# Attention on TensorE: the transposes of each block of probabilities are handed out one at a time between long products, from a queue, and the products with the values follow from it

## The chip, the cores and the metric

The kernel runs on one core of one Trainium2 chip. The metric is the device time of one execution in microseconds (us), lower is better. One execution was also taken with the hardware profiler; all rows below come from that one.

## The reference

Two layers of a decoder over 512 tokens of width 1024. A layer has five attention branches (each four heads of 64), a gate per branch, an output projection with a layer norm, and a mixture of 16 experts.

```
...
    h = x @ w_in
...
    o_sb = merge_heads(stick_breaking_attention(heads(q, N_SB_HEADS), heads(k, N_SB_HEADS), heads(v, N_SB_HEADS)))
...
    o_moba = merge_heads(moba_attention(heads(q, N_MOBA_HEADS), heads(k, N_MOBA_HEADS), heads(v, N_MOBA_HEADS),
                                        alibi_slopes(N_MOBA_HEADS)))
    o_mla = mla_attention(c_q, c_kv, k_rope_in, g_cq, g_ckv, w_uq, w_ukv)
    o_nsa = nsa_attention(heads(q_nsa, N_NSA_HEADS), kv_nsa, g_nsa, nsa_pe, w_phi_k1, w_phi_k2, w_phi_v1, w_phi_v2,
                          alibi_slopes(N_NSA_HEADS))
    o_mem = memory_cross_attention(q_mem, mem, w_mem_kv)
    merged = jnp.zeros_like(x)
    for i, o in enumerate((o_sb, o_moba, o_mla, o_nsa, o_mem)):
        gate = jax.nn.sigmoid(x @ w_gate[i] + b_gate[i])
        merged = merged + gate * (o @ w_br[i])
    return merged @ w_out
```

Four of the branches end in a softmax over the scores, times the values; stick-breaking attention has products of `1 - sigmoid` along the row in the softmax's place.

## The kernel before, in words

**Numbers.** Every matrix product is made of three products: each operand is split into a high part, rounded to the fast 32-bit format of TensorE, and a low part that holds the rest. ScalarE (ACT) makes the high part, `hi` (L97 is its plain copy), and VectorE (DVE) the low one, `lo` (L112). Tiles of the program are named by their tag: `xh`, `xl` are the two parts of the residual stream, `wh` those of a weight, `oh` those of a branch's output, `bh` those of its projection.

**A head.** In each branch a head has four blocks of 128 queries. `score_block` (L239) multiplies queries and keys into a PSUM bank `s` (there are two). DVE adds the distance term and takes the row's minimum into an SBUF tile `ne` (L254; there are three of them, `BUFS["ne"]`), ACT takes the exponential (L259), DVE the reciprocal of the sum (L260) and the scaling (L262, or L264 with a gate). Where there is no distance term, the minimum is read from `s` and the exponential goes from `s` to `ne`. Stick-breaking uses two `ne` tiles for each block: a mask (L425), tanh on ACT (L427), a linear step (L428), a scan along the row (L432) and a difference (L433), back in the first tile.

**Turns.** `to_pt` (L267) then turns the block over, since the product with the values needs the keys on the partitions: one transpose of 128x128 for every 128 keys (L124, `tr`), one to four a block, into a PSUM bank `pt` (two). I call such a transpose a turn. ACT's copy into `pth` (L97) and DVE's difference into `ptl` (L112) split the bank. When a head's four blocks are turned, `causal_pv` multiplies them with the values into the one PSUM bank `pv`, and `pv_out` adds its two halves (L280 on ACT, L281 on DVE).

**The order.** A head alone would leave TensorE waiting for DVE and ACT, so each of the five stages (memory, stick-breaking, MoBA, MLA, NSA) weaves three generators: `a`, the attention of this branch, a step for each query block; `g`, the gates and the projection of the branch before (L780 to L800: gate product `f<-xh,wh` from `fm_tile` L166, then `f<-oh,bh`); and `q`, the queries, keys and values of the branch behind. A string of letters for each stage (`orders`, L1642) says whose turn it is, and `weave` (L867) calls them. That is the order in which the program is written. A list scheduler then emits, for each engine, the instruction that is ready by its own estimate, with the place in the written order as its priority. So each engine's order comes out of the scheduler, and every engine executes its own in order.

There are 472 turns of `ne` blocks in the two layers.

Of the kernel before, what the change touches and what calls it, by code (L numbers as in the profile page):

```python
# [18 lines left out]
P = 128  # L19
D = 1024  # L20
S = 512
NT = 4
KT = 8
# [47 lines left out]
class Trunk:  # L71
    def __init__(self, tc, A, C, out, dbg=None, upto=None):
        self.tc, self.nc, self.A, self.C, self.out = tc, tc.nc, A, C, out
        self.dbg, self.upto = dbg or {}, upto
        self.uid = 0

    def nm(self, s):
# [36 lines left out]

    def mm(self, out, lhsT, rhs, start, stop):
        self.nc.tensor.matmul(out, lhsT, rhs, start=start, stop=stop)  # L116

# [41 lines left out]
    def fm_tile(self, wh, wl, M=P, N=S, x=None, cut=1):  # L159
        o = self.ps("f")  # L160
        xh, xl = (self.xh, self.xl) if x is None else x
        for c in range(cut):
            n = slice(c * N // cut, (c + 1) * N // cut)
            for k in range(KT):
                for m, (a, b) in enumerate(((wh, xh), (wh, xl), (wl, xh))):
                    self.nc.tensor.matmul(o[:M, n], a[:, k, :M], b[:, k, n], start=c + k + m == 0, stop=k == KT - 1 and m == 2,  # L166
                                          skip_group_check=cut > 1)
        return o
# [8 lines left out]
    def tm_chunk(self, w, c0, use, x=None, nt=NT, outer="k"):  # L177
# [5 lines left out]
        def part(g, kk, t):  # L183
            if g not in hl:
                hl[g] = self.split_w(self.load_w(w[512 * g : 512 * g + 512, c0 : c0 + 256].rearrange("(k p) c -> p k c", p=P), (4, 256)))
            h, l = hl[g]
            k = 4 * g + kk
            sl = slice(t * P, (t + 1) * P)
            d = o[t // 2][:, 256 * (t % 2) : 256 * (t % 2) + 256]
            for m, (a, b) in enumerate(((xh, h), (xh, l), (xl, h))):  # L190

                self.nc.tensor.matmul(d, a[:, k, sl], b[:, kk, :], start=k == 0 and m == 0 and t % 2 == 0,  # L192
                                      stop=k == KT - 1 and m == 2, skip_group_check=True)
        its = [(g, kk) for g in range(2) for kk in range(4)]
# [120 lines left out]
    def causal_head(self, passes, vt, strip=0, slope=1.0):  # L315
        pt = self.pt_tiles()
        for i in range(NT):
# [3 lines left out]
            yield  # L321
        pv = self.ps("pv")
        self.causal_pv(pv, pt, vt, True, True)
        return pv

# [47 lines left out]
    def mem_att(self, l, out):  # L373
        for pr in range(2):
            o32 = self.o_tile()
            out.append(o32)
            for hh in range(2):
# [7 lines left out]
                pv = self.ps("pv")  # L385
                for j in range(2):
                    for m in range(2):
                        self.mm(pv[:, :S], self.mv[j][:, h, :], pt[m][:, 512 * j : 512 * j + 512], j == 0 and m == 0, j == 1 and m == 1)
                self.pv_out(pv, o32, self.H2[hh])
                yield  # L390
# [19 lines left out]
    def sb_att(self, l, out):  # L410
        nc = self.nc
        for pr in range(2):
            o32 = self.o_tile()
            out.append(o32)
            for hh in range(2):
# [3 lines left out]
                for i in range(NT):  # L419
# [15 lines left out]
                    yield  # L435
                pv = self.ps("pv")
                self.causal_pv(pv, pt, lambda j: self.sv[j][:, h, :], True, True)
                self.pv_out(pv, o32, self.H2[hh])
                yield
# [16 lines left out]
    def moba_att(self, l, out):  # L456
        for pr in range(2):
            o32 = self.o_tile()
            out.append(o32)
            for hh in range(2):  # L460
                h = 2 * pr + hh
                q, k = self.bq[h], self.bk[h]
                pv = yield from self.causal_head(self.std_passes(q, k), lambda j: self.bv[j][:, h, :], 0, SLOPES[h])
                self.pv_out(pv, o32, self.H2[hh])
                yield
            self.dump(f"o_moba{pr}_{l}", o32)
# [132 lines left out]
    def mla_att(self, l, out):  # L599
        for pr in range(2):  # L600
            o32 = self.o_tile()
            out.append(o32)
            for hh in range(2):
# [5 lines left out]
                          (lambda sl: qb[K, sl], lambda sl: ka[K, sl])]  # L609
                pv = yield from self.causal_head(passes, lambda j: self.lv[j][:, h, :], 1)  # L610
                self.pv_out(pv, o32, self.H2[hh])
                yield
# [106 lines left out]
    def nsa_att(self, l, out):  # L719
# [32 lines left out]
        for pr in range(2):  # L752
            o32 = self.o_tile()
            out.append(o32)
            for hh in range(2):
# [3 lines left out]
                for m in range(2):  # L759
# [6 lines left out]
                    pts.append(pt)  # L766
                pv = self.ps("pv")
                self.mm(pv, self.vc[:, h, :], pc[:, 0, :], True, False)
                self.mm(pv, self.vc[:, h, :], pc[:, 1, :], False, False)
                for m in range(2):  # L770
                    self.causal_pv(pv, pts[m], lambda j, m=m: self.nv[j][:, m, :], False, m == 1)
                self.pv_out(pv, o32, self.H2[hh])
                yield
# [91 lines left out]

    @staticmethod
# [729 lines left out]
    def layer(self, l, gat, att):  # L1596
# [8 lines left out]
        with tc.tile_pool(name=f"pre{l}", bufs=1, reuse_waits="tile") as pre:  # L1605
# [6 lines left out]
            with tc.tile_pool(name=f"exp{l}", bufs=1, reuse_waits="tile") as ep:  # L1612
# [103 lines left out]
```

## Time and profile before

| | |
|---|---|
| median of 3 runs | 1697.85 us (1696.06, 1697.85, 1702.87) |
| the profiled execution | 1704.54 us, its span 1702.7 us |
| granted TensorE clock, mean | 0.972 of full speed |
| attention of layer 0, of layer 1 | about 75 to 600 us, 890 to 1440 us of the span |
| experts of layer 0, of layer 1 | the rest, from 600 and from 1440 us |

The span is the profiler's stretch from the first instruction to the last. Times within it are counted from its start. A row of the timeline is one instruction, or several of a kind in a row ("x4"), with its start, its length, and in square brackets how long its engine sat idle before it and whose work ended that. The end of a product on TensorE is modelled, and includes the time that the last columns take through the array: the next product starts before it. So what a product costs in a stream is read from start to start.

### The profile page before, as it was taken

To read this page: it belongs to the slowest core of one execution; us is meant where nothing else is said; L and a number is where in the kernel's file an instruction comes from. 1 tells how busy PE (TensorE), PEld (TensorE's weight loads), DVE (VectorE), ACT (ScalarE), POOL (GpSimd) and SP (SyncE) were. 2 spreads that over 40 slices of the span, in tenths; PEclk is the share of its full clock that TensorE was granted. 3 is DMA by queue.
4 is the path that set the end of the run, shared out by engine and by line. 5 is a ranking of instruction groups with operands and counts; after the bars stand their busy time and mean duration, and the time that the engine had idled before them with its cause. 6 is when DMAs were issued, how large, how long until landed. Compare 5 with 4: busy or idle time off the path is not lost. (4 is left out here: it accounts for less than half of the span.)

```text
span 1702.7 us, 22755 instructions
## 1 busy us (share of the span) xinstructions
PE 1603.2 (94%) x7936; PEld 1271.8 (75%) x7936; DVE 1253.3 (74%) x2551; ACT 867.3 (51%) x1655; POOL 272.7 (16%) x218
## 2 busy tenths in 40 slices
PE   8999999999999998899699999999999999989995
PEld 7877877788777786666587778777877787766673
DVE  6777658764785689988788766588557956898887
ACT  5644446343463335788346444464344624358871
POOL 0000011111112112333300000111101121223332
PEclk9999999989999998999799999999999999999997
DMA  8232222434328747997541323223332285499954
GB/s 254 64 91 77 67 71 61 119 95 124 106 79 281 255 165 282 378 379 251 195 141 52 94 73 81 66 62 98 79 88 63 58 305 183 170 326 380 381 178 156
DMA packets 254563, 273.61 MB, mean 161 GB/s; under 512 B 38666, under 2 KB 191360, under 8 KB 254432
## 3 DMA queue, kind: packets, MB, share of 16 engines
q1 hardware_dynamic: 241032, 223.98, 41.3%
q0 software_dynamic: 13312, 47.98, 8.2%
q8 instruction: 67, 1.10, 0.3%
q14 instruction: 64, 0.52, 0.1%
q10 hardware_dynamic: 88, 0.03, 0.0%
HBM read 239.18 MB, written 32.77 MB: 160 GB/s over the span
## 5 line engine op out<-in xcount | busy, mean ns | idle before, releaser
L166 PE MATMUL f<-xh,wh 128*128 128x512 f32 (+2 forms) x1920 | 631.0, 397 | 2.0 <-DVE ot L592 1.1
L166 PEld LDWEIGHTS f<-xh,wh 128*128 128x128 f32 (+1 forms) x1920 | 355.7, 189 | 77.0 <-PE f L625 1.2
L166 PE MATMUL f<-xl,wh 128*128 128x512 f32 (+2 forms) x960 | 381.1, 397 | 0.0
L112 DVE TENSOR_TENSOR wh<-rw,wh 128x1024 fp32r<-128x1024 f32 (+1 forms) x174 | 227.5, 1313 | 51.5 <-ACT wh L97 50.4
L798 POOL TENSOR_TENSOR mg<-mg,gt 128x512 f32<-128x512 f32 x64 | 96.8, 1512 | 986.1 <-DVE gt L797 986.1
L166 PEld LDWEIGHTS f<-xl,wh 128*128 128x128 f32 (+1 forms) x960 | 181.0, 188 | 36.7 <-DVE xl L112 0.2
L97 ACT CAST wh<-rw 128x1024 fp32r<-128x1024 f32 (+3 forms) x178 | 178.5, 1012 | 52.6 <-PE f L192 14.9
L788 ACT ACTIVATE gt<-f,bgh 128x512 f32<-128x512 f32 x80 | 55.0, 688 | 211.8 <-PE f L166 211.8
L116 PE MATMUL f<-wh,xh 128*112 128x512 f32 (+1 forms) x564 | 153.9, 400 | 1.9 <-DVE wh L112 1.9
L116 PE MATMUL f<-oh,bh 128*128 128x512 f32 x480 | 132.5, 403 | 0.1
L797 DVE SCALAR_TENSOR_TENSOR gt<-gt,f 128x512 f32<-128x512 f32 x64 | 43.8, 684 | 107.3 <-PE f L116 102.8
L116 PEld LDWEIGHTS f<-wh,xh 128*112 128x112 f32 (+1 forms) x564 | 98.3, 178 | 31.8 <-DVE wh L112 3.3
L97 ACT CAST pth<-pt 128x128 fp32r<-128x128 f32 (+1 forms) x192 | 77.4, 417 | 87.2 <-PE pt L124 81.5
L116 PE MATMUL f<-eh,xh 128*112 128x512 f32 (+1 forms) x396 | 110.5, 401 | 0.9 <-DVE eh L112 0.8
L112 DVE TENSOR_TENSOR ptl<-pt,pth 128x128 fp32r<-128x128 f32 (+1 forms) x192 | 88.9, 473 | 24.7 <-ACT pth L97 21.8
L116 PEld LDWEIGHTS f<-oh,bh 128*128 128x128 f32 x480 | 89.8, 191 | 20.0 <-issue 1.2
L116 PE MATMUL s<-qk,qk 128*128 128x256 f32 (+7 forms) x416 | 99.2, 336 | 5.9 <-DVE st L254 2.6
L97 ACT CAST wh<-rp 128x1024 fp32r<-128x1024 f32 x84 | 87.5, 1053 | 30.9 <-PE pt L116 16.3
L112 DVE TENSOR_TENSOR wh<-rp,wh 128x1024 fp32r<-128x1024 f32 x70 | 95.4, 1374 | 8.4 <-ACT wh L97 7.8
L124 PE MATMUL pt<-ident,ne 128*128 128x128 f32 x472 | 83.7, 279 | 8.6 <-DVE ne L433 3.8
L116 PEld LDWEIGHTS s<-qk,qk 128*128 128x128 f32 (+1 forms) x416 | 67.5, 194 | 26.9 <-DVE st L254 9.3
L124 PEld LDWEIGHTS pt<-ident,ne 128*128 128x128 f32 x472 | 54.7, 141 | 42.4 <-issue 17.1
(355 smaller groups left out, 2756.4 us busy)
## 6 DMA issues: line engine op xcount, KB each, us to landing
rp<-in_w_up_dram SPq DMA_DIRECT2D x96, 512.0 KB, 14.4
rw<-in_w_gate_dram SPq DMA_DIRECT2D x80, 512.0 KB, 3.8
rp<-in_w_down_dram SPq DMA_DIRECT2D x48, 512.0 KB, 13.6
rw<-in_w_in_dram SPq DMA_DIRECT2D x38, 512.0 KB, 3.8
rw<-in_w_out_dram SPq DMA_DIRECT2D x32, 512.0 KB, 6.5
yd<-xl POOLq DMA_DIRECT2D x28, 448.0 KB, 6.8
xl<-xd POOLq DMA_DIRECT2D x24, 448.0 KB, 7.5
rb<-in_w_br_dram SPq DMA_DIRECT2D x80, 128.0 KB, 3.3
```

What stands on the lines that cost most here:

```text
L97: return nc.scalar.copy(out, in_)
L112: return e.tensor_tensor(out, in_, hi.bitcast(F32), ALU.subtract)
L116: self.nc.tensor.matmul(out, lhsT, rhs, start=start, stop=stop)
L124: return self.nc.tensor.transpose(out, in_, self.ident[:k, :k])
L166: self.nc.tensor.matmul(o[:M, n], a[:, k, :M], b[:, k, n], start=c + k + m == 0, stop=k == KT - 1 and m == 2, skip_group_check=cut > 1)
L788: nc.scalar.activation(t, gp, AF.Tanh, bias=self.bgh[:, b * 8 + f : b * 8 + f + 1], scale=0.5)
L797: nc.vector.scalar_tensor_tensor(t, t, 1.0, bp, ALU.add, ALU.mult)
L798: i = nc.gpsimd.tensor_tensor(m, m, t, ALU.add)
```

## The change

Products now count. All that had called TensorE directly goes through `mm`, and each product of 256 columns or more (`long`) adds one to a count (`tick`). `to_pt` no longer emits a block's turns: it puts each into a queue (`later`). The first one of a block becomes due 20 long products after it was queued (`delay`), each further one 2 long products behind the one ahead of it (`space`), and after the last one of a block of nb the queue rests for max(1, 10 - 2(nb - 1)) (`gap_t`). The split into `pth` and `ptl` is issued with the last turn. The products with the values are closures (`end`, `out`) in the same queue, so they follow the turns they need. `weave` empties the queue at the end of each stage. Nothing else is computed, and the number of instructions is the same. The strings of `orders` and the scheduler stay.

```diff
-    def mm(self, out, lhsT, rhs, start, stop):
-        self.nc.tensor.matmul(out, lhsT, rhs, start=start, stop=stop)
+    def mm(self, out, lhsT, rhs, start, stop, **kw):
+        i = self.nc.tensor.matmul(out, lhsT, rhs, start=start, stop=stop, **kw)
+        if rhs.shape[-1] >= self.long:
+            self.big = i
+            self.tick()
+    def tick(self):
+        if self.busy:
+            return
+        self.now += 1
+        while self.pend and max(self.pend[0][0], self.due) <= self.now:
+            if self.do_next():
+                break
+    def do_next(self):
+        _, gap, f = self.pend.pop(0)
+        self.busy = True
+        f()
+        self.busy = False
+        self.due = self.now + gap
+        return gap
+    def flush(self):
+        while self.pend:
+            self.do_next()
+    def later(self, f, gap=0, delay=0):
+        self.pend.append((self.now + delay, gap, f))
...
     def to_pt(self, e, nb, dst):
-        t = self.ps("pt")
+        h, l = dst
+        ts = []
+        def turn(b):
+            if b == 0:
+                ts.append(self.ps("pt"))
+            t = ts[0]
+            if True:
+                self.tr(t[:, b * P : (b + 1) * P], e[:, b * P : (b + 1) * P])
+            if b == nb - 1:
+                src = t[:, : nb * P].rearrange("p (b q) -> p b q", q=P)
+                self.hi(h, src)
+                self.lo(l, src, h)
         for b in range(nb):
-            self.tr(t[:, b * P : (b + 1) * P], e[:, b * P : (b + 1) * P])
-        src = t[:, : nb * P].rearrange("p (b q) -> p b q", q=P)
-        h, l = dst
-        self.hi(h, src)
-        self.lo(l, src, h)
+            self.later(lambda b=b: turn(b), self.space if b < nb - 1 else max(1, self.gap_t - self.space * (nb - 1)), 0 if b else self.delay)
...
-                pv = self.ps("pv")
-                self.causal_pv(pv, pt, lambda j: self.sv[j][:, h, :], True, True)
-                self.pv_out(pv, o32, self.H2[hh])
+                def end(h=h, hh=hh, pt=pt, o32=o32):
+                    pv = self.ps("pv")
+                    self.causal_pv(pv, pt, lambda j: self.sv[j][:, h, :], True, True)
+                    self.pv_out(pv, o32, self.H2[hh])
+                self.later(end)
...
-    def weave(parts, order):
+    def weave(self, parts, order):
         for c in order:
             next(parts[c], None)
         for g in parts.values():
             for _ in g:
                 pass
+        self.flush()
...
+    busy = False
+    long, delay, space, gap_t = 256, 20, 2, 10
```

**What moves on TensorE.** The scheduler still reorders, so the order that comes out of it is shown at three places. Numbers behind a tag tell tiles of one tag apart.

The first place is the MoBA stage of layer 0, the third and fourth query block of a head, before the change. `s_2095` and `s_2110` are their scores, `ne_2098` and `ne_2113` their probabilities, `f_2145` a gate's product. Rows 7 and 8 below are this place in the trace.

```order
L116 MATMUL s_2095<-qk_1536,qk_1135 128x384
L116 MATMUL s_2110<-qk_1535,qk_1135 128x512
L116 MATMUL s_2110<-qk_1536,qk_1135 128x512
L116 MATMUL f_2126<-oh_2052,bh_2060 128x512 x3
L116 MATMUL f_2126<-oh_2055,bh_2060 128x512 x3
...
L166 MATMUL f_2145<-xh_102,wh_2142 128x512
L124 MATMUL pt_2104<-ident,ne_2098 128x128 x3
L166 MATMUL f_2145<-xh_102,wh_2142 128x512
L166 MATMUL f_2145<-xl_103,wh_2142 128x512
L124 MATMUL pt_2119<-ident,ne_2113 128x128 x4
L166 MATMUL f_2145<-xh_102,wh_2142 128x512 x2
```

The same two blocks with the change; their probabilities are now `ne_2093` and `ne_2104`, the gate's product is `f_2132`, and `ne_2037` is the block ahead.

```order
L117 MATMUL s_2099<-qk_1518,qk_1135 128x512
L154 MATMUL pt_2102<-ident,ne_2037 128x128
L117 MATMUL f_2110<-oh_2043,bh_2051 128x512 x2
L154 MATMUL pt_2102<-ident,ne_2037 128x128
...
L117 MATMUL f_2132<-xh_102,wh_2129 128x512
L154 MATMUL pt_2145<-ident,ne_2093 128x128
L117 MATMUL f_2132<-xh_102,wh_2129 128x512
L117 MATMUL f_2132<-xl_103,wh_2129 128x512
L154 MATMUL pt_2145<-ident,ne_2093 128x128
L117 MATMUL f_2132<-xh_102,wh_2129 128x512 x2
...
L154 MATMUL pt_2161<-ident,ne_2104 128x128
```

Where three and four turns stood in a lump, each now stands alone with one to three long products behind it. From the last score of the fourth block to that block's first turn there were 17 long products and 3 turns; now there are 28 and 5.

The second place is the stick-breaking stage of layer 0, before the change: the fourth score of a head and the turns near it.

```order
L116 MATMUL pv_1299<-ptl_1187,v_591 128x128
L124 MATMUL pt_1324<-ident,ne_1317 128x128
L116 MATMUL s_1361<-qk_960,qk_672 128x512
L116 MATMUL s_1361<-qk_961,qk_672 128x512
L166 MATMUL f_1401<-xh_102,wh_1398 128x512
L166 MATMUL f_1401<-xl_103,wh_1398 128x512
L124 MATMUL pt_1339<-ident,ne_1332 128x128 x2
```

The same score, `s_1323`, with the change. `ne_1225` is the block of 512 keys of the head ahead.

```order
L154 MATMUL pt_1357<-ident,ne_1225 128x128
L117 MATMUL f_1345<-xh_102,wh_1342 128x512 x2
L154 MATMUL pt_1357<-ident,ne_1225 128x128
...
L154 MATMUL pt_1357<-ident,ne_1225 128x128
L117 MATMUL f_1345<-xh_102,wh_1342 128x512
L117 MATMUL s_1323<-qk_917,qk_662 128x512
L117 MATMUL s_1323<-qk_918,qk_662 128x512
L117 MATMUL f_1345<-xh_102,wh_1342 128x512
```

The turns of a head's last block now run on until the scores of the next head are under way. Its `ne` tile comes free with the last of them, and one long product behind that stands a score that needs the bank which tanh empties into that tile.

The third place is the end of the NSA stage of layer 0, before the change. `pv_4943` is the stage's last product with the values; `oh_5013` and `oh_5016` are the outputs of its two pairs of heads, `oh_4015` one of the MLA stage.

```order
L116 MATMUL pv_4943<-ptl_4827,v_3813 128x128
L166 MATMUL f_4975<-xl_103,wh_4972 128x512
...
L166 MATMUL f_4975<-xh_102,wh_4972 128x512
L116 MATMUL f_5002<-oh_4015,bh_4967 128x512 x3
...
L116 MATMUL f_5056<-oh_5013,bh_5021 128x512 x3
L116 MATMUL f_5056<-oh_5016,bh_5021 128x512 x3
```

And with the change.

```order
L154 MATMUL pt_4977<-ident,ne_4717 128x128 x3
L154 MATMUL pt_4983<-ident,ne_4730 128x128 x4
L117 MATMUL f_5075<-xh_102,wh_5072 128x512 x2
...
L117 MATMUL pv_4990<-ptl_4692,v_3813 128x128
L117 MATMUL f_5075<-xh_102,wh_5072 128x512
L117 MATMUL f_5102<-oh_5013,bh_5067 128x512 x3
L117 MATMUL f_5121<-xh_102,wh_5118 128x512
...
L117 MATMUL f_5056<-oh_5016,bh_5021 128x512
L117 MATMUL f_5102<-oh_5016,bh_5067 128x512
```

The last turns come out in lumps where the queue is emptied. The last product with the values stands later among the gates' products, and 11 long products lie between it and the first that uses the second pair's output, where there were 44.

## Rows read from the trace of the kernel before

**Rows 1.** Page: busy time and share of the span, by engine.
```profile
PE 1603.2 (94%) x7936; PEld 1271.8 (75%) x7936; DVE 1253.3 (74%) x2551; ACT 867.3 (51%) x1655; POOL 272.7 (16%) x218
```

**Rows 2.** Windows, both layers' attention: length, PE, PEld, DVE, ACT, POOL busy, clock, DMA share.
```profile
75.00:600.00 525.00, 513.99 (x2487) 410.88 (x2485) 354.36 (x771) 243.77 (x525) 62.32 (x50) 0.99 0.39 116
890.00:1440.00 550.00, 540.12 (x2644) 431.69 (x2643) 375.63 (x820) 260.74 (x567) 52.24 (x33) 0.99 0.34 102
```

**Rows 3.** Tile pt, all engines: the turns, and what PE sat idle for.
```profile
L124 PE MATMUL pt<-ident,ne x472: 270/273/332, 52.1 to 1358.7; 128*128 128x128 f32 x158
...
  DVE ne L433: 3.8, 12
  DVE ne L262: 2.8, 6
```

**Rows 4.** Waits of PE, 75 to 600 us: engine, line, from whom: total us, times, longest.
```profile
PE s L116 <- ACT ne L259: 1.4, 1, 1.4
PE s L116 <- DVE st L254: 1.3, 3, 0.8
...
PE s L116 <- ACT ne L427: 0.4, 1, 0.4
```

**Rows 5.** Page, costliest groups: the score products: busy, mean | idle before.
```profile
L116 PE MATMUL s<-qk,qk 128*128 128x256 f32 (+7 forms) x416 | 99.2, 336 | 5.9 <-DVE st L254 2.6
```

**Rows 6.** Timeline of PE: one turn and four turns between long products, no wait.
```profile
84.66 0.63 PE L166 MATMUL f<-xh,wh 128*128 128x512 f32 x2
85.12 0.60 PE L124 MATMUL pt<-ident,ne 128*128 128x128 f32 x4
85.48 0.48 PE L166 MATMUL f<-xl,wh 128*128 128x512 f32 x1
85.79 0.39 PE L166 MATMUL f<-xh,wh 128*128 128x512 f32 x1
...
244.50 0.63 PE L166 MATMUL f<-xh,wh 128*128 128x512 f32 x2
244.97 0.27 PE L124 MATMUL pt<-ident,ne 128*128 128x128 f32 x1
245.00 0.48 PE L166 MATMUL f<-xl,wh 128*128 128x512 f32 x1
245.31 0.63 PE L166 MATMUL f<-xh,wh 128*128 128x512 f32 x2
```

**Rows 7.** Timeline of PE, MoBA stage of layer 0: scores to turns of two blocks.
```profile
209.80 1.55 PE L116 MATMUL f<-oh,bh 128*128 128x512 f32 x6
...
213.85 0.39 PE L166 MATMUL f<-xl,wh 128*128 128x512 f32 x1
215.03 0.63 PE L124 MATMUL pt<-ident,ne 128*128 128x128 f32 x4 [0.80 <-DVE ne L262]
```

**Rows 8.** Timeline of VectorE, the same place.
```profile
210.02 0.69 DVE L254 CUSTOM_DVE_ANT_0 ne<-s,strip 128x512 f32<-128x512 f32 x1
...
213.05 1.44 DVE L112 TENSOR_TENSOR bh<-rb,bh 128x256 fp32r<-128x256 f32 x1
214.41 0.47 DVE L262 TENSOR_SCALAR ne<-ne,st 128x512 f32<-128x512 f32 x1
```

**Rows 9.** Timeline of PE, stick-breaking stage of layer 0: a score and turns that wait.
```profile
114.13 0.62 PE L116 MATMUL s<-qk,qk 128*128 128x384 f32 x2 [0.38 <-ACT ne L427]
...
120.03 0.52 PE L124 MATMUL pt<-ident,ne 128*128 128x128 f32 x3 [0.28 <-DVE ne L433]
```

**Rows 10.** Waits of VectorE, 30 to 600 us, the one for a turned `ne` tile.
```profile
DVE ne L254 <- PE pt L124: 0.8, 1, 0.8
```

**Rows 11.** Timeline of PE, end of the MLA stage: last values product, first use of its output.
```profile
432.19 0.27 PE L116 MATMUL pv<-ptl,v 128*128 128x128 f32 x1
...
433.97 0.75 PE L116 MATMUL s<-kc,qk 128*128 128x64 f32 x6
434.78 0.50 PE L116 MATMUL f<-oh,bh 128*128 128x512 f32 x1
```

More of the change, by code (lines that the diff above doesn't have):

```diff
@@ L75, in __init__ @@
         self.uid = 0
+        self.pend, self.now, self.due, self.big = [], 0, 0, None
     def nm(self, s):
@@ L165, in fm_tile @@
                 for m, (a, b) in enumerate(((wh, xh), (wh, xl), (wl, xh))):
-                    self.nc.tensor.matmul(o[:M, n], a[:, k, :M], b[:, k, n], start=c + k + m == 0, stop=k == KT - 1 and m == 2,
-                                          skip_group_check=cut > 1)
+                    self.mm(o[:M, n], a[:, k, :M], b[:, k, n], c + k + m == 0, k == KT - 1 and m == 2, skip_group_check=cut > 1)
         return o
@@ L190, in part @@
             for m, (a, b) in enumerate(((xh, h), (xh, l), (xl, h))):
-                self.nc.tensor.matmul(d, a[:, k, sl], b[:, kk, :], start=k == 0 and m == 0 and t % 2 == 0,
-                                      stop=k == KT - 1 and m == 2, skip_group_check=True)
+                self.mm(d, a[:, k, sl], b[:, kk, :], k == 0 and m == 0 and t % 2 == 0, k == KT - 1 and m == 2, skip_group_check=True)
         its = [(g, kk) for g in range(2) for kk in range(4)]
@@ L321, in causal_head, with out @@
             yield
-        pv = self.ps("pv")
-        self.causal_pv(pv, pt, vt, True, True)
-        return pv
+        def out(use):
+            pv = self.ps("pv")
+            self.causal_pv(pv, pt, vt, True, True)
+            use(pv)
+        return lambda use: self.later(lambda: out(use))
     def std_passes(self, q, k):
@@ L384, in mem_att @@
                     yield
[L385 to L388, printed above, removed]
-                self.pv_out(pv, o32, self.H2[hh])
+                def end(h=h, hh=hh, pt=pt, o32=o32):
+                    pv = self.ps("pv")
+                    for j in range(2):
+                        for m in range(2):
+                            self.mm(pv[:, :S], self.mv[j][:, h, :], pt[m][:, 512 * j : 512 * j + 512], j == 0 and m == 0, j == 1 and m == 1)
+                    self.pv_out(pv, o32, self.H2[hh])
+                self.later(end)
                 yield
@@ L435, in sb_att, with end @@
                     yield
-                pv = self.ps("pv")
-                self.causal_pv(pv, pt, lambda j: self.sv[j][:, h, :], True, True)
-                self.pv_out(pv, o32, self.H2[hh])
+                def end(h=h, hh=hh, pt=pt, o32=o32):
+                    pv = self.ps("pv")
+                    self.causal_pv(pv, pt, lambda j: self.sv[j][:, h, :], True, True)
+                    self.pv_out(pv, o32, self.H2[hh])
+                self.later(end)
                 yield
@@ L462, in moba_att @@
                 q, k = self.bq[h], self.bk[h]
-                pv = yield from self.causal_head(self.std_passes(q, k), lambda j: self.bv[j][:, h, :], 0, SLOPES[h])
-                self.pv_out(pv, o32, self.H2[hh])
+                pv = yield from self.causal_head(self.std_passes(q, k), lambda j, h=h: self.bv[j][:, h, :], 0, SLOPES[h])
+                pv(lambda x, o32=o32, hh=hh: self.pv_out(x, o32, self.H2[hh]))
                 yield
@@ L609, in mla_att @@
                           (lambda sl: qb[K, sl], lambda sl: ka[K, sl])]
-                pv = yield from self.causal_head(passes, lambda j: self.lv[j][:, h, :], 1)
-                self.pv_out(pv, o32, self.H2[hh])
+                pv = yield from self.causal_head(passes, lambda j, h=h: self.lv[j][:, h, :], 1)
+                pv(lambda x, o32=o32, hh=hh: self.pv_out(x, o32, self.H2[hh]))
                 yield
@@ L766, in nsa_att, with end @@
                     pts.append(pt)
[L767 to L772, printed above, removed]
+                def end(h=h, hh=hh, pts=pts, o32=o32):
+                    pv = self.ps("pv")
+                    self.mm(pv, self.vc[:, h, :], pc[:, 0, :], True, False)
+                    self.mm(pv, self.vc[:, h, :], pc[:, 1, :], False, False)
+                    for m in range(2):
+                        self.causal_pv(pv, pts[m], lambda j, m=m: self.nv[j][:, m, :], False, m == 1)
+                    self.pv_out(pv, o32, self.H2[hh])
+                self.later(end)
                 yield
@@ L864, in x_tile @@
             self.lo(self.xl[:, 4 * g : 4 * g + 4, t * P : (t + 1) * P], v, h)
-    @staticmethod
-    def weave(parts, order):
+    def weave(self, parts, order):
         for c in order:
```

## The prediction, made before the changed kernel was run

> **What bounds the kernel now.** I read the page first: TensorE is busy for 94% of the span, no other engine for more than 74% [rows 1]. So only two things can shorten this kernel, fewer products, which the change doesn't bring, or less time in which TensorE stands still. Where it stands still is read next, from the windows of the two attention stretches, the only stages that the change touches: 525.0 - 514.0 = 11.0 us idle in layer 0 and 550.0 - 540.1 = 9.9 us in layer 1 [rows 2]. That is all there is to win at first sight, some 21 us of 1704.54. DVE is not full there either (354 of 525 us).
>
> Then what it stands still for. The answer on the tile pt gives the turns: 12 waits for the stick-breaking block (DVE L433), 3.8 us, and 6 for a scaled softmax block (L262), 2.8 us [rows 3]. The waits of layer 0 give the scores, which wait for a PSUM bank until the step that reads it has run: 1.4 + 1.3 + 0.4 us in 5 waits [rows 4]; in the whole run the scores stand behind 5.9 us of idle time [rows 5]. One block shows why a turn waits. Its scores are through when the next products start, at 209.80, and its probabilities are scaled at 214.41 + 0.47 = 214.88: 5.1 us, of which 1.44 is a split of a weight that DVE has in between [rows 8]. The order had put only 17 long products and 3 turns between (first place), 4.3 us at the cadence below, so TensorE idles for 0.80 us [rows 7].
>
> **The price of a turn itself.** Two long products start 0.47 us apart from the next thing, 0.235 each: 244.50 to 245.31 is 0.81 us for three of them and one turn, so the turn costs 0.11. Four turns in a lump: 84.66 to 85.79 is 1.13 us with three long products, so 0.43, again 0.11 each [rows 6]. A turn alone is no cheaper and no dearer than in a lump. So splitting the lumps as such I cost at nothing (472 turns, 0 us); what counts is where the turns stand against the work that they wait for.
>
> The Trainium skill (TensorE: Matmul & The Clock Gate, "Step-by-step" and "LDWEIGHTS") says that TensorE loads the next weights beneath the product that runs, and gives the load of 128 columns some 107 ns. By that a single turn between two long products would hide its load, and the sum would be lower, as in the last rival below. The 0.11 us of the turn at 244.97, which stood alone, speaks against it.
>
> **Part by part.**
>
> *Turns later.* What waits cost is more than their idle time, since a product's end is modelled late: the turn due at 213.85 + 0.235 = 214.08 starts at 215.03, 0.95 us late for 0.80 idle [rows 7]. With 0.15 more for each, the 18 waits are worth 6.6 + 18 x 0.15 = 9.3 us [rows 3]; that is the lower bound of what turns lose. For the upper one I went through the timeline run by run, start to start, as with the rows above: 166 runs of adjacent turns, 452 turns, the first at 52.1 and the last at 1358.7 us [rows 3], take 71.8 us beyond the products beside them, against 452 x 0.109 = 49.3: 22.5 us of delay, most of it too short to show as idle time.
>
> How much of it goes is a matter of the order. I counted, for all 196 score blocks with a turn, the products between the end of the scores and the first turn, at the cadence of the rows: the median rises from 4.7 to 7.8 us, and runs of one turn from 36 to 246. In the block shown it goes from 17 to 28 long products, 4.3 to 7.1 us, against a chain of 5.1. A quarter of the blocks does less well, since the scheduler puts a turn early where its estimate says it is ready, and lumps stay where the queue is emptied (third place). Taking for each kind of block the median chain that the timelines show (2.9 to 6.3 us), the sum of what the turns come too early falls from 43 to 16.5 us over both layers, and with chains 15% longer from 111 to 33: 62 to 70% goes. I take 60%, since a turn no longer late lets DVE and ACT meet other work, and apply it to the upper bound, because that was measured by starts and holds the lower one: **-13.5 us**; the ends are 0.62 x 9.3 = -6 and 0.70 x 22.5 = -16.
>
> *Tiles and banks held longer.* A turn that comes later holds its `ne` tile for longer, and there are three. A score block whose tile isn't free can't be read out, so its bank `s` stays full and the score after next waits. In the order 37 of 98 blocks of a layer had a tile that was freed only after their own scores; with the change 60. In the second place a score stands one long product behind the turn that frees the tile which its bank has to be emptied into; such a wait was 0.38 us before [rows 9]. Summed as above, what scores come too early grows from 16.0 to 25.6 us, by 60%. What scores lose now is 5.9 us of idle [rows 5] and, for some 10 waits, 0.15 each, so 7.4; 60% of that is **+4 us**. The ends are 0 (the tile is freed before DVE gets there) and the rival below. The bank `pt` is held for longer too, from a block's first single turn to its split; the queue rests after each block, and I cost this at nothing; without that cover it would come out as a wait of the turns, in the ends above.
>
> *Products with the values, and stage ends.* They follow the turns, so the output of a stage's last head is ready later, and the first projection that reads it stands 2.3 to 2.6 us behind the last value product in three stages instead of 2.3 to 10 (third place: 11 long products, 44 before). The trace has such a place: 432.30 to 434.78 is 2.5 us, and there the projection starts 0.15 us after its place in the stream, 433.97 and six scores of 0.11 [rows 11]. Ten stage ends in all: 0 to 1.5 us; I take **+0.5**.
>
> *What is queued behind.* ACT's copy of a turned block now stands with its last turn; behind it on ACT stand exponentials and weight splits. TensorE has work of the gates meanwhile, and I cost it at nothing. The loads on SP and POOL come out in the same number and nearly the same order, and DMA is busy for 0.39 of the time in these stretches [rows 2]: nothing.
>
> **The sum** against the profiled execution: 1704.54 - 13.5 + 4 + 0.5 = 1695.5 us. That execution is 6.7 us above the median of the runs shown, 1697.85; the difference of -9.0 carried over to the median gives **1688.9 us**. A change of 0.5%, 8.5 us, is about what a measurement of this kernel can tell from none, so the forecast is at its edge.
>
> **Rivals.** *Waits only change place.* TensorE gets the turns without a wait, but the chain of DVE and ACT is no shorter, and each score that comes after a held tile gives back what a turn gained. For it speaks the order (37 to 60 held blocks), against it that DVE has slack in attention. Gain of turns -13.5, scores as much: 1698 us.
>
> *Everything falls into place.* Turns gain their upper end, 16, and the scores, no longer delayed by a head that ran late, lose their 7.4 as well: 1697.85 - 23 = 1675. For it speaks that turns and scores wait for the same chain of DVE steps; against it the second place.
>
> *Three tiles are too few (slower).* The 46 more held blocks (23 in each layer) wait in DVE's queue for their tile, with everything behind them, and the scores at 0.62 us each, the mean of the five waits of layer 0 [rows 4]: +28.5, less 13.5, so 1713. It decides from the point where some 22 of the 46 wait at that price, 22 x 0.62 = 13.5. For it speaks the one wait of DVE for a turned tile, 0.8 us [rows 10]; against it that 37 held blocks a layer made only that one. The Trainium skill (same page, its table of the engine's figures) says that VectorE and ScalarE take their queues strictly in order, only TensorE draws loads ahead; so a wait for a tile would hold all that DVE has behind it, as this rival assumes.
>
> *The weight load hides.* A turn alone costs its own columns only, 0.235 x 128/512 = 0.06: 472 x 0.05 = 24 us more, 1665. The row of the lone turn speaks against it [rows 6].
>
> *The change doesn't do what it says*, since the scheduler moves turns back: the order excludes it, 246 single turns for 36.
>
> **How the numbers follow.** The forecast's own case 0.55, from 1682 to 1700 by its bounds; a little over half of it lies beyond 8.5 us of gain (0.30), the rest within (0.25). Waits that change place 0.20 (0.16 within, 0.04 slower). Everything falls into place 0.12. Three tiles too few 0.09 (slower). The hidden load 0.04. So faster 0.30 + 0.12 + 0.04 = 0.46, the same 0.25 + 0.16 = 0.41, slower 0.13. The range goes from 1674 to 1703: it leaves out the hidden load, most of the slower case and the tails, under 2 in 10.
>
> **What would show it.** Right: turns x1 in the timeline, the idle time before them from DVE L433 and L262 at about a third of 6.6 us, attention's PE idle time at 6 to 8 us a layer in place of 11.0 and 9.9, the scores' idle time at 8 to 10 us. Wrong: idle time before turns as before (the chains grew with the order), or a long row of waits of DVE L254 or ACT L427 for turned tiles, with scores waiting behind them.

## The result, and the profile after

The changed kernel is slower: median 1714.50 us (1713.49 to 1717.24, 5 runs) against 1697.85 us (1695.56 to 1702.87, 5 runs), a ratio of 1.0096 with a 95% interval of 1.0075 to 1.0117. The forecast was 1688.9 us and the range ended at 1703. The profiled execution took 1714.27 us.

The page shows what the two groups of rows at stake became: first the scores, then the turns (busy, mean of one | idle before, and what ended most of it).

```profile
L117 PE MATMUL s<-qk,qk 128*128 128x256 f32 (+7 forms) x416 | 102.0, 344 | 13.6 <-ACT ne L287 6.1
L154 PE MATMUL pt<-ident,ne 128*128 128x128 f32 x472 | 106.1, 278 | 6.0 <-DVE ne L290 2.4
```

In the page of the kernel before, the turns had this line:

```profile
L124 PE MATMUL pt<-ident,ne 128*128 128x128 f32 x472 | 83.7, 279 | 8.6 <-DVE ne L433 3.8
```

The turns gained 2.6 us of idle time (8.6 before), and the scores lost 7.7 (5.9 before, [rows 5]). What ends the idle time of turns changed too: from the answer on the tile pt,

```profile
  DVE ne L290: 2.4, 2
  DVE ptl L113: 1.9, 4
...
  DVE ne L475: 0.6, 2
```

so the 12 waits for the stick-breaking block are down to 2, and the 6 for a scaled block to 2 [rows 3]. Their idle time is 3.0 us in place of 6.6, where a third, 2.2, was forecast. In their place stand waits for DVE's `ptl`, which has to empty a bank `pt`.

The windows of the two attention stretches, to be read against [rows 2]: TensorE's busy time, the second figure, falls by 2.6 and 4.3 us.

```profile
75.00:600.00 525.00, 511.40 (x2458) 404.51 (x2457) 354.84 (x762) 242.85 (x523) 62.26 (x49) 0.99 0.38 114
890.00:1440.00 550.00, 535.78 (x2623) 425.22 (x2621) 373.13 (x812) 258.88 (x565) 52.73 (x33) 0.99 0.33 96
```

The waits of TensorE's scores, 75 to 600 us, to be read against [rows 4]: 9 where there were 5.

```profile
PE s L117 <- ACT ne L287: 2.7, 2, 1.4
PE s L117 <- ACT ne L469: 1.6, 3, 0.9
PE s L117 <- DVE st L282: 1.4, 3, 0.7
...
PE s L117 <- DVE ne L781: 0.5, 1, 0.5
```

The place of [rows 7, 8] did what was wanted. Its block of 512 keys, on TensorE and VectorE:

```profile
212.37 1.12 DVE L290 TENSOR_SCALAR ne<-ne,st 128x512 f32<-128x512 f32 x1
```
```profile
215.42 0.63 PE L117 MATMUL f<-xh,wh 128*128 128x512 f32 x2
215.89 0.27 PE L154 MATMUL pt<-ident,ne 128*128 128x128 f32 x1
215.92 0.48 PE L117 MATMUL f<-xl,wh 128*128 128x512 f32 x1
216.23 0.41 PE L117 MATMUL f<-xh,wh 128*128 128x512 f32 x1
216.47 0.27 PE L154 MATMUL pt<-ident,ne 128*128 128x128 f32 x1
```

No wait; but the block is ready at 213.49, and its first turn starts 2.4 us later. For that time, and until its fourth turn, it holds one of three tiles. What that does is seen on VectorE and ScalarE: their waits for a turn, 75 to 600 us (total, times, longest).

```profile
DVE ne L282 <- PE pt L154: 7.1, 8, 2.0
```
```profile
ACT pth L98 <- PE pv L117: 12.9, 8, 3.1
...
ACT ne L287 <- PE pt L154: 7.5, 5, 2.6
...
ACT ne L469 <- PE pt L154: 4.7, 3, 2.8
```

Before, the first was one wait of 0.8 us [rows 10], the last two didn't exist, and the second was

```profile
ACT pth L97 <- PE pv L116: 0.6, 2, 0.4
```

One place of the NSA stage shows such a wait and how far it reaches: VectorE,

```profile
484.64 0.42 DVE L282 CUSTOM_DVE_ANT_0 ne<-s,strip 128x256 f32<-128x256 f32 x1 [1.35 <-PE pt L154]
486.11 0.56 DVE L282 CUSTOM_DVE_ANT_0 ne<-s,strip 128x384 f32<-128x384 f32 x1 [0.40 <-PE pt L154]
...
488.48 0.69 DVE L845 SCALAR_TENSOR_TENSOR gt<-gt,f 128x512 f32<-128x512 f32 x1 [0.21 <-PE f L117]
...
489.16 1.20 DVE L113 TENSOR_TENSOR wh<-rw,wh 128x1024 fp32r<-128x1024 f32 x1
490.28 1.45 DVE L292 TENSOR_SCALAR ne<-ne,st,gate 128x384 f32<-128x384 f32 x1
...
491.72 0.27 DVE L282 CUSTOM_DVE_ANT_0 ne<-s,strip 128x128 f32<-128x128 f32 x1
```

and TensorE:

```profile
483.18 0.27 PE L154 MATMUL pt<-ident,ne 128*128 128x128 f32 x1
...
483.76 0.27 PE L154 MATMUL pt<-ident,ne 128*128 128x128 f32 x1
...
484.33 0.27 PE L154 MATMUL pt<-ident,ne 128*128 128x128 f32 x1
...
492.05 0.62 PE L117 MATMUL s<-qk,qk 128*128 128x384 f32 x2 [0.67 <-DVE st L282]
```

Three turns come one by one with long products between. VectorE stands for 1.35 us until the last has freed the tile, then for 0.40 at the next. TensorE's products from 484.3 to 488.4 start 0.45 us late in sum, two scores among them by 0.11 and 0.16 us, too little each to show as idle time. At 488.48 VectorE waits for a gate's product, so by then it has caught up with TensorE. At 492.05 a score waits 0.67 us for a bank that VectorE reads at 491.72; ahead of that stand a weight's split of 1.20 us and a scaling that takes 1.45 us, so this wait can't be put down to the three turns. That held tiles reach the scores is shown by e1 below, not by this place.

**Where the time went.** I took for each product of the two attention stretches (75 to 610 and 890 to 1450 us) the time to the start of the next one, less its own time in the stream (0.232 us for 512 columns, 0.175 for 384, 0.117 for 256, 0.110 below), and put it down to the next one's tile. The second profile of the kernel before (e5, below), which lies at its median, has 57.0 us of such delay, the changed one 72.9: the difference of 15.9 is that of their spans, 1712.5 - 1696.6. So all of the loss lies in the attention stretches; the measure counts a product that runs at TensorE's low clock as delay too:

| delay before, us, both layers | scores | turns | values | rest |
|---|---|---|---|---|
| kernel before (e5) | 14.2 | 19.3 | 3.6 | 19.9 |
| changed | 29.8 | 15.2 | 5.2 | 22.7 |

By stage (from the start of its first gate's activation to that of the next stage; NSA's reaches on to the third gate behind it, and up to the first one it is 7.6 us in the changed kernel), per layer, mean of both:

| us | stick-breaking | MoBA | MLA | NSA |
|---|---|---|---|---|
| before (e5) | 6.0 | 6.4 | 7.7 | 5.5 |
| changed | 4.8 | 8.0 | 11.3 | 8.9 |
| changed, four `ne` tiles (e1) | 4.5 | 7.3 | 12.1 | 6.2 |
| before, four `ne` tiles (e2) | 6.2 | 6.4 | 6.7 | 5.0 |
| changed, no rest (e4) | 5.1 | 4.7 | 8.4 | 6.9 |

Stick-breaking gains 1.2 us; the three stages behind it lose 8.6. Part of that is TensorE's clock, of which more is told after the experiments. The profiler's record of the granted clock has two levels; split by the level at which a product starts, the delays of attention, both layers, are:

| us | spent at the low level | delay in it | delay outside it |
|---|---|---|---|
| before (e5) | 10.2 | 5.1 | 51.9 |
| changed | 27.3 | 14.2 | 58.7 |
| changed, four `ne` tiles (e1) | 30.7 | 16.0 | 51.3 |
| before, four `ne` tiles (e2) | 6.8 | 2.8 | 51.4 |
| changed, no rest (e4) | 10.2 | 5.0 | 52.9 |

So of the 15.9 us, 6.8 are delay outside the low stretches (scores +10.5, turns -4.8, the rest +1.1) and 9.1 lie in them, where TensorE runs slower and stands as well. The growth of the MLA column lies in the low stretches alone.

### The profile page after: what moved, and what is told of

Same layout as the page of the kernel before. It is cut to its first block, busy times and chain, and to the rows that moved or that the text cites. A ratio compares the mean times of both kernels' runs of the same rounds, so it can differ in the third digit from the quotient of the medians.

```text
span 1712.5 us, 22775 instructions
## 1 busy us (share of the span) xinstructions
PE 1605.9 (94%) x7936; PEld 1265.7 (74%) x7936; DVE 1253.4 (73%) x2551; ACT 866.7 (51%) x1655; POOL 273.3 (16%) x218
## 5 line engine op out<-in xcount | busy, mean ns | idle before, releaser
L117 PE MATMUL f<-xh,wh 128*128 128x512 f32 (+2 forms) x1920 | 637.9, 400 | 3.8 <-DVE ot L637 1.1
L113 DVE TENSOR_TENSOR wh<-rw,wh 128x1024 fp32r<-128x1024 f32 (+1 forms) x174 | 222.8, 1284 | 46.2 <-ACT wh L98 44.9
L117 PE MATMUL f<-wh,xh 128*112 128x512 f32 (+2 forms) x820 | 202.0, 364 | 5.5 <-DVE wh L113 4.1
L117 PEld LDWEIGHTS f<-wh,xh 128*112 128x112 f32 (+1 forms) x820 | 138.7, 182 | 37.0 <-DVE wh L113 6.1
L154 PE MATMUL pt<-ident,ne 128*128 128x128 f32 x472 | 106.1, 278 | 6.0 <-DVE ne L290 2.4
L117 PEld LDWEIGHTS f<-oh,bh 128*128 128x128 f32 x480 | 87.3, 191 | 22.7 <-issue 1.2
L154 PEld LDWEIGHTS pt<-ident,ne 128*128 128x128 f32 x472 | 60.9, 141 | 33.0 <-issue 11.9
## 6 DMA issues: line engine op xcount, KB each, us to landing
rp<-in_w_up_dram SPq DMA_DIRECT2D x96, 512.0 KB, 14.2
rp<-in_w_down_dram SPq DMA_DIRECT2D x48, 512.0 KB, 13.2
```

The source lines that it names most:

```text
L113: return e.tensor_tensor(out, in_, hi.bitcast(F32), ALU.subtract)
L117: i = self.nc.tensor.matmul(out, lhsT, rhs, start=start, stop=stop, **kw)
L154: return self.nc.tensor.transpose(out, in_, self.ident[:k, :k])
```

## The experiments

Two theories stood at the start against a third. A: turns that come later hold the three tiles, and scores wait. B: the spreading itself costs (banks `pt`, ScalarE at the copy). C: the queue, which gives each block some 10 long products, falls behind the blocks, so the turns come much later than the delay of 20 says; a tenth of the blocks has 13.9 us of products and more between scores and first turn.

**e1, a fourth tile.**
```diff
-    BUFS = dict(rb=2, bh=2, gt=2, oo=4, oh=2, qk=18, v=6, ne=3, ...
+    BUFS = dict(rb=2, bh=2, gt=2, oo=4, oh=2, qk=17, v=6, ne=4, ...
```


> The changed kernel with a fourth ne tile (one spare qk tile given up for it, which alone leaves every engine's order as it is). Theory A, tiles held by late turns make the scores wait: the changed trace shows some 30 us of delay in front of scores against 15 before, and most of the added 15 should go, so 1714 falls to about 1697 to 1702, and the waits of DVE L282 and ACT L287 for a turn vanish. Theory B, the cost lies in the spreading itself (banks pt held, ACT waiting at the split's copy): no change, 1710 to 1717. Theory C, the queue falls behind and everything behind it is late: a small gain, 1705 to 1712, since the turns stay as late.

1707.15 us (1705.04 to 1708.26), ratio 1.0057 (1.0043 to 1.0071). The delay of scores falls from 29.8 to 21.4 us, and VectorE's waits for a turn to half:

```profile
DVE ne L282 <- PE pt L154: 3.8, 5, 1.5
```

ScalarE's wait at L287, which A wanted gone too, stays (7.5 before it):

```profile
ACT ne L287 <- PE pt L154: 8.2, 4, 3.0
```

About half of the loss goes, less than A wanted: the held tiles are a part of it. What is left is at the low clock: outside the low stretches the delay is back to that of the kernel before (51.3 against 51.9 us), but 30.7 us are spent in them. Four of this run's five executions have a mean clock of 0.972, the median of the kernel before is 0.977.

**e2, the same tile in the kernel before** (the same edit).

> The control: the kernel before with the same fourth ne tile. Theory A: the kernel before holds its tiles for a short time only and gains little, 1692 to 1698. B and C: no change, 1696 to 1700. If it gains as much as the changed kernel does, the tile is not the cause of the loss but a gain of its own.

1695.02 us, ratio 0.9984 (0.9970 to 0.9997): 2.9 us of gain, against 7.4 in the changed kernel. The tile is worth more where turns are late, as A says, and something on its own.

**e3, delay without spreading.**
```diff
-    long, delay, space, gap_t = 256, 20, 2, 10
+    long, delay, space, gap_t = 256, 20, 0, 10
```


> The changed kernel with space 0: a block's turns are due together after 20 long products, and the queue still rests for 10 after each block. 36 single turns again, as before the change, but the median distance from scores to first turn stays at 7.4 us. Theory A and C, lateness costs: as slow as the change, 1711 to 1718. Theory B, spreading costs: back to 1696 to 1702 or better.

1710.93 us (1705.59 to 1712.05), ratio 1.0073 (1.0058 to 1.0088). With the turns in lumps again 13.0 of 16.6 us of the loss stay, so B falls as the main cause. The intervals of this and the change overlap; whether spreading costs a little can't be told.

**e4, no rest.**
```diff
-    long, delay, space, gap_t = 256, 20, 2, 10
+    long, delay, space, gap_t = 256, 20, 2, 1
```


> The changed kernel with gap_t 1: turns 2 long products apart and first due after 20, but no rest between blocks, so that the queue doesn't fall behind; the median distance from scores to first turn falls from 7.8 to 5.6 us and the longest tenth from 13.9 to 7.5. Theory C, the backlog of the queue: most of the loss goes, 1695 to 1702. Theory A: about half goes, 1702 to 1708, since tiles are held for less long. Theory B: 166 single turns remain of 246, so little goes, 1708 to 1715.

1700.30 us (1693.61 to 1703.73, 12 runs), ratio 1.0018 (1.0005 to 1.0032): 14 of 16.6 us come back. The delay of 20 and the spacing of 2 are still there; only the pause behind each block is gone. The waits for a turn, VectorE and ScalarE:

```profile
DVE ne L282 <- PE pt L154: 1.1, 2, 0.8
```
```profile
ACT ne L469 <- PE pt L154: 5.3, 4, 2.8
ACT ne L287 <- PE pt L154: 3.3, 4, 1.7
```

The delay of scores is 17.0 us, that of turns 21.1, against 14.2 and 19.3 in the kernel before: without the pause the queue neither gains nor loses much. The time at the low clock is that of the kernel before again, 10.2 us, and 9.2 of the 14.9 us of delay that come back between the two profiles lay in the low stretches. So the pause costs both waits and clock.

**e5, the kernel before, profiled again.**

> The kernel before, profiled once more, since its first profile (1704.54 us) lay 6.7 us above its median. If that was TensorE's clock, this one lies near 1698 us and shows some 5 to 14 us at half clock in the two attention stretches in place of 23.9, with the same waits. If it was waits, the idle time before turns and scores differs between the two profiles by several us.

1698.34 us. The delays of turns and scores, 19.3 and 14.2, are near those of the first profile, 19.2 and 15.1. The windows around the 32 products of 31 columns in the MLA stage (350 to 400, 1150 to 1240 us) show the difference; the first profile,

```profile
350.00:400.00 50.00, 49.59 (x226) 40.60 (x225) 25.43 (x51) 16.90 (x42) 11.29 (x10) 0.90 0.49 129
1150.00:1240.00 90.00, 87.53 (x424) 71.09 (x423) 61.30 (x133) 35.97 (x87) 12.51 (x8) 0.94 0.33 87
```

and this one:

```profile
350.00:400.00 50.00, 49.54 (x238) 40.72 (x237) 27.70 (x55) 19.19 (x45) 11.29 (x10) 0.97 0.50 133
1150.00:1240.00 90.00, 87.08 (x434) 70.78 (x433) 60.84 (x132) 35.40 (x86) 12.07 (x8) 0.98 0.34 89
```

The granted clock (third figure from the end) is a mean of the two levels, 1.2 and 2.4 GHz. (1 - clock) x 2 x length gives 10.0 + 10.8 = 20.8 us at the low one before, and 3.0 + 3.6 = 6.6 here; the spans differ by 6.1. So the first profile was an execution with a low clock.

**e6, the queue off in the MLA stage; e7, in the NSA stage.** Both set the three numbers by stage; e6 is shown, in e7 the last entry is the one at zero.
```diff
+    modes = ((20, 2, 10), (20, 2, 10), (20, 2, 10), (0, 0, 0), (20, 2, 10))
...
+            self.delay, self.space, self.gap_t = self.modes[n]
             self.weave(parts, self.orders[n])
```


> The changed kernel, with the queue at delay 0, space 0 and gap_t 0 in the MLA stage alone (its turns follow their scores as before, and the values' products follow them). The 32 products of 31 columns lie in this stage, behind which the clock falls to half for 10 us in both layers. Theory of the clock (late turns and waiting scores around these short products make it fall in every execution): the time at half clock in attention goes from 27 us to 14 or less, and with the stage's extra score delay of about 6 us gone as well the time falls by 8 to 14, to 1701 to 1707. Theory of held tiles alone: only the score delay goes, 1707 to 1711, and the clock falls as before.

1713.17 us, with executions from 1701.46 to 1717.10. The profiled one was the shortest; its MLA stage took 5.7 us of delay a layer in place of 11.3. By its median nothing was gained, which neither theory gave; by this profile 13 us. See e12 to e14.

> The same with the queue off in the NSA stage alone, where two thirds of the score blocks lie. Theory of held tiles: the stage's score delay goes from 4.2 us a layer to the 1.7 of the kernel before, its turns from 3.6 to 2.9, so 1707 to 1711, at the same clock. Theory of the backlog carried from stage to stage: it is emptied at every stage's end, so no more than this. If the loss lay here alone, 1698 to 1702.

1707.10 us (1705.32 to 1711.22), ratio 1.0053 (1.0034 to 1.0072). The delay in NSA falls from 8.9 to 6.3 us a layer, as A and C expected: 2 x 2.6 of the 7.4 us that the median fell.

**e8, no rest and a fourth tile** (the edits of e4 and e1).

> No rest in the queue (gap_t 1) and a fourth ne tile. If the backlog and the held tiles are two causes, their remedies add: 1700 less 3 to 7, so 1692 to 1697, below the kernel before and near its version with four tiles (1695). If both remedies take away the same waits, 1698 to 1702.

1696.66 us (1693.60 to 1703.97), ratio 1.0000 (0.9985 to 1.0015). That is inside the range for two causes, but the tile gives 3.6 us here, near the 2.9 of e2 and not the 7.4 of e1: most of what it mended in e1, the missing pause has mended already. And the whole only comes back to the kernel before: with late turns mended, the queue is worth nothing over all stages.

**e9, the values' products alone in the queue; e10, the rest alone.**
```diff
-    long, delay, space, gap_t = 256, 20, 2, 10
+    long, delay, space, gap_t = 256, 0, 0, 0
```


> The queue with delay 0, space 0 and gap_t 0 everywhere: a block's turns are handed out in a lump at the next long product, as before, and only the products with the values (and the writing order) go through the queue. 38 single turns, median distance from scores to turns 4.7 us as before. If the values' products that follow cost something, slower than 1700; if all of the loss comes from late turns, the same as before, 1696 to 1700.

1698.38 us, ratio 1.0016 (1.0004 to 1.0027): the products with the values and the writing order cost 1.5 us by the medians, 0.7 to 4.6 by the interval.

```diff
-    long, delay, space, gap_t = 256, 20, 2, 10
+    long, delay, space, gap_t = 256, 0, 2, 10
```


> delay 0, space 2, gap_t 10: the first turn of a block may go at once, but the queue rests for 10 after each block. The median distance is 5.6 us, as without the rest and with the delay of 20 (e4, 1700), but the longest tenth stands at 11.6 us in place of 7.5. Theory of the backlog (the tail costs, not the delay): 1704 to 1710. If the delay of 20 is what costs, 1696 to 1700.

1704.58 us, ratio 1.0056 (1.0039 to 1.0073). With no delay at all, the rest makes it slower by 7.7 us, while delay and spacing without the rest (e4) cost 2.4, and both together 16.6. So the delay alone is not what costs, but with the rest it costs another 9. Loss and longest tenth rise together (7.5 us in e4, 11.6 here, 13.9 in the change), as C says. That held tiles are how it costs (A) is shown for a part only, by e1.

**e11, the queue in two stages.** Four tiles, and the queue where the table by stage says that it gains.
```diff
+    modes = ((0, 0, 0), (20, 2, 10), (20, 2, 1), (0, 0, 0), (0, 0, 0))
```


> Four ne tiles, the queue as changed in the stick-breaking stage, without rest in the MoBA stage, and off (delay 0, space 0, gap_t 0) in the other three. By the stages of the traces so far TensorE's delay is 4.5 us in stick-breaking with the queue and four tiles (6.1 without), 4.6 in MoBA without rest (6.4), and no better with the queue in the others. If stages can be put together, 2 x 3.4 = 7 us go from the kernel before with four tiles (1695): 1687 to 1690. If what a stage gains is given back in the next one, 1693 to 1697.

1690.51 us (1685.67 to 1696.24, 12 runs), half a microsecond above what was expected, ratio to the kernel before 0.9955 (0.9941 to 0.9968): faster than both, and than the kernel before with four tiles. Stick-breaking takes 4.4 us of delay a layer and MoBA 4.7, as in the runs they were taken from. The waits for an `ne` tile that had grown are gone or small (VectorE, then ScalarE, 75 to 600 us; ScalarE has no other for an `ne` tile), and that for `pth` is down from 12.9 to 4.5 us:

```profile
DVE ne L282 <- PE pt L154: 0.8, 1, 0.8
```
```profile
ACT ne L469 <- PE pt L154: 1.3, 3, 0.7
```

**e12, e13, e14: the kernel of e6 three more times, and e15, the change again,** to see what the clock does.

> The kernel of e6 once more, for a second profile: its six executions lay between 1701.5 (the profiled one, 3.4 us at half clock in attention) and 1717. Theory of the clock: if this execution is a long one, near 1713, its waits are those of the first profile and the difference lies in stretches at half clock. If its waits differ, by the transfers or the scores, the clock isn't the reason.

> A third look at the kernel of e6, whose executions spread over 16 us. Theory of the clock: a long execution (over 1708 us) has the same waits by stage as the two short ones profiled, and 15 us or more of further time at half clock in one of the attention stages. If a long one shows other waits at the same clock, the spread has another cause. A short one (under 1704) tells nothing new.

> A fourth look at the kernel of e6, with the expectations of the third: a long execution differs by its time at half clock (theory of the clock) or by its waits (another cause); a short one tells nothing new.

1703.30, 1712.96 and 1715.94 us. The two windows of the MLA stage in e6's first profile (1701.46),

```profile
350.00:400.00 50.00, 48.95 (x244) 40.14 (x243) 27.53 (x54) 18.82 (x42) 11.28 (x10) 1.00 0.53 141
1150.00:1240.00 90.00, 87.11 (x442) 71.02 (x441) 62.53 (x135) 37.35 (x89) 12.76 (x8) 1.00 0.35 92
```

and in e13 (1712.96):

```profile
350.00:400.00 50.00, 49.54 (x224) 40.59 (x225) 25.88 (x53) 16.89 (x41) 11.27 (x10) 0.90 0.48 125
1150.00:1240.00 90.00, 86.52 (x412) 69.96 (x411) 62.24 (x139) 35.42 (x86) 10.40 (x7) 0.92 0.31 82
```

None at the low clock in the first, 10.0 + 14.4 = 24.4 us in the second, which is 11.5 us longer. In the other four stages their delays agree within 0.2 us, but for the second MoBA stage of the short one (8.8 against 7.2), which had 3.4 us at the low clock. The same program, the same waits, another clock: that explains the difference of these two executions. It doesn't explain all of e6's spread. e14, with 13.8 us of it in MLA and more in MoBA, has 23.9 us at the low level in attention where e13 has 27.3, and is 3 us longer; and an execution of e6 that wasn't profiled took 1713.14 us at a mean clock of 0.976, where the shortest had 0.979, a difference worth some 5 of 11.7 us by the prices at the end.

> A second profile of the changed kernel, whose five executions lay within 4 us. Theory of the clock: again some 24 us or more at half clock in attention, in both layers around the products of 31 columns, and a time of 1712 to 1718. If it falls to 10 us or less and the time is still 1712 or more, the clock has no part in the loss.

1715.85 us, and in the two windows 0.90 and 0.96, so 10.0 + 7.2 us, and 0.87 from 312 to 350 us, 9.9 us more; the delay of turns and scores is 15.4 and 26.6 us. The expected 24 us or more are met only with these.

## Why the prediction was wrong

*What bounds the kernel* held in part: all 15.9 us of difference lie in the attention stretches, but only some 7 to 10 of them are TensorE standing; the others are its clock, for which the sum had no term.

*The price of a turn* held. The lone turns in the profile after cost 0.11 us each in the median, so spreading as such is worth nothing to TensorE, and the rival of the hidden load fell.

*Turns later, -13.5 us:* mis-sized. Their delay went from 19.3 to 15.2 us, -4.1. In stick-breaking it all but vanished (4.2 to 0.9 us a layer), in NSA it grew (2.2 to 2.9). I had counted how many products stand between scores and turns, and set that against chains of fixed length; that the chains got longer, since VectorE and ScalarE now stood waiting for tiles with the next block's work behind them, is how I read it, and no run measured it.

*Tiles and banks held longer, +4 us:* this is the step that failed. The scores lost 15.6 us more, 10.5 of it outside the low stretches. I had the count right (37 to 60 held blocks) and took for the price what scores lost before, times 1.6; the rows of one wait of DVE in the trace of before [rows 10] said nothing of how far the new tail of 13.9 us would reach. The rival of three tiles named the mechanism and, at 1713, nearly the time, with a chance of 0.09. That its time is so near is luck: its terms were +28.5 and -13.5, measured were +15.6 and -4.1, and the clock makes up much of the sum. Its 46 waits of 0.62 us are not what happened either: VectorE and ScalarE stood 7.1 + 7.5 + 4.7 = 19.3 us in layer 0 in 16 waits for a turn, and TensorE's waits of scores rose only from 5 to 9, 0.7 us each, with many delays too short to show as idle time. The Trainium skill (TensorE: Matmul & The Clock Gate, the table of the engine's figures) says that those two take their queues strictly in order. The trace agrees in that nothing else starts on VectorE in the 1.35 us before 484.64; but what stands behind comes late only until 488.48.

*Products with the values, +0.5:* they lost 1.6 us, most of it in the low stretches; e9 leaves 0.7 to 4.6.

*What is queued behind, nothing:* not as I took it. ScalarE waits 12.9 us, where it was 0.6, to write `pth` until the head ahead has been multiplied with the values. I hadn't looked at how many tiles `pth` has: it is one. What these waits cost TensorE stays open, since no run gave `pth` a second tile; they are 13.2 us in e1 and 6.3 in e4.

*The carry from the profile to the median* was a second step that failed. I subtracted 6.7 us without asking why the profiled execution was above the median. It was TensorE's clock, at 0.972; the median executions of the kernel before have 0.977 (0.973 to 0.980), those of the change 0.972 (0.971 to 0.975). So the change runs nearly always at the clock of the slowest executions before. Compared at the same clock, the two first profiles, it costs 9.8 us of span; the other 6 or so up to 15.9 are the clock (the split by level gives 6.8 outside the low stretches and 9.1 in them). The loss of clock goes with the pause: without it (e4) the median execution has 0.975, with it 0.972. Why stays open. That late turns and waiting scores around the short products bring the clock down wasn't shown: with the queue off in that stage (e6, e12 to e14) it fell in some executions and not in others.

## What to carry to other kernels

Work that is put off holds whatever it was to free. Before delaying a step, count the buffers behind it and take the longest delay that the schedule gives, not the median: a queue with a fixed pause per item must be faster than the items arrive. Look stage by stage; the same rule gained 1.2 us in one stage and lost 3.4 in another, and put on only where it gains, with a fourth tile, it beat both kernels. And before a profile's time is carried to a median, compare their clocks.

## What the runs showed that I had not expected

One program spreads over 16 us (1701.5 to 1717.1), in large part by TensorE's clock. It falls in the middle of a busy stage; the longest low stretches of attention stand around 32 products of 31 columns in a row. In the changed kernel:

```profile
355.94 3.67 PE L117 MATMUL f<-ne,rw 128*128 128x31 f32 x32
359.54 0.42 PE L117 MATMUL f<-gel,kt 128*64 128x32 f32 x2
359.89 1.33 PE L154 MATMUL pt<-ident,ne 128*128 128x128 f32 x5
360.87 2.16 PE L117 MATMUL s<-qk,qk 96*128 96x512 f32 x6
```

The five turns behind take (360.87 - 359.89) / 5 = 0.20 us each where they take 0.11 at the full clock. In the profiles at hand it stayed low for 0 to 24 us in the two MLA stages together, and each us at the low clock cost 0.43 us (e5 against the first profile, 6.1 of 14.2) to 0.47 us (e13 against e6, 11.5 of 24.4), if the whole difference of the spans is put down to it. The delays in attention alone give 0.36 (5.0 of 13.7 us) to 0.43 (10.2 of 23.9).
